# A residual loaded two tiles ahead, low-half products last in a chunk, and new figures in a build's own estimate

## The chip, the cores and the metric

The kernel runs on one core of one Trainium2 chip. Its time is the device time of one execution in microseconds (us), as the median of several runs. The profile is one further execution, recorded by the hardware profiler. TensorE (PE) does the matrix products, with its weight loads shown apart (PEld); VectorE (DVE), ScalarE (ACT) and GpSimd (POOL) do the elementwise work, and SyncE (SP) issues the transfers.

## The reference

Two blocks follow each other on 512 tokens of 2048 channels, all in float32. The first has a state-space branch, a differential attention and an attention to 256 memory tokens:

```python
h = rmsnorm(x, norm_pre); proj = h @ w_in            # 2048 -> 5120
y_s = gated(s5_scan(u_s, ...)); y_d = diff_attention(...) * silu(g_d)
y_x = memory_attention(q_x, mem_n, w_mem_kv) * silu(g_x)
mix = concatenate([y_s, y_d, y_x]) @ w_out
x = x + rmsnorm(mix, norm_post)
```

The last line is the residual that the change loads earlier. The second block has two layers over these 512 latent tokens and 256 context tokens; both streams use the same weights, and the attention of the latent tokens reads the keys of both:

```python
h = rmsnorm(x, g) * (1 + scale) + shift; hc = rmsnorm(xc, g) * (1 + scale_c) + shift_c
q, k, v, pool, fourier, gate = split(h @ w_in)       # q and k normalised and rotated
out = concatenate([attention, pool, fourier]) * silu(gate) @ w_out
x = x + gate_ada * out                               # and the context alike, in layer 0
return rmsnorm(x, final_norm_g)
```

## The kernel before, in words

Activations lie with channels on the partitions, as 16 tiles of 128 x 512 (or 128 x 256 for the context and the memory). A product in float32 is made of three products in a reduced format: each operand is split into a high half, which is a cast, and a low half, which is the rest (`hi`, `lo`). The three are hi x hi, hi x lo and lo x hi. In the profile `whi` and `wlo` are the halves of a weight chunk of 128 x 512, which serves four contraction tiles, and `hh` and `hl` are the halves of an activation tile. ScalarE casts `whi`, VectorE subtracts to get `wlo`; the chunk comes by DMA into `raw`. `gemm` (line 515) makes one output tile of 128 channels from two or four chunks, 12 matmuls each, into the PSUM tile `mm`. There are 912 chunks in a plan made at the start, and a chunk is split up to three chunks ahead of its use (`wsplit`, `wahead`).

All other work is written as generators, which run beside the products. Between matmuls `gemm` calls `tick`; `tick` advances each generator whose time has come on a clock of the build's own. This clock is not the chip's: `count` (line 286) adds to it an estimate for each instruction as it is recorded, from the table `COST` (line 217: a fixed part and a part per element for each engine) and a formula for matmuls. So the estimates set after how many products a step of other work stands in each engine's program. Each engine works its own program in that order; an instruction whose input is late holds up those behind it. Nothing of this clock is in the built program.

Steps that the text speaks of: `post` (line 1716) belongs to the second block. After the first block's output product it normalises the 16 output tiles, adds the residual (`xr`, loaded from `xT`), stores each tile (`x1d`) and scales it for layer 0. It runs beside the context products of layer 0. `attn_out` (line 846) transposes the softmax rows `P` into a PSUM tile `tp`, splits them into `pth` and `ptl`, and multiplies by the values into `pv`. `g_rope` (line 808) rotates queries and keys: four copies of 32 rows on ScalarE, then products on VectorE with the table `axial`. A read of one row in the profile always names line 210, where every operation is recorded; tiles tell the rows apart.

Of the kernel before, what the change touches and what calls it, by code (L numbers as in the profile page):

```python
# [22 lines left out]
N = 512  # L23
# [190 lines left out]

class Build:

    COST = {"vector": (0.08, 0.00106), "scalar": (0.09, 0.00084), "gpsimd": (0.15, 0.0021),
            "sync": (0.1, 0.00125), "tensor": (0.0, 0.0)}
    SLACK = 0.1
    CALM, LIMIT = 2.0, 3.6  # L220
# [5 lines left out]
    def __init__(self, tc, I, out):  # L226
        self.tc, self.I, self.out = tc, I, out
        self.nc = SimpleNamespace(**{e: Engine(self, e) for e in self.COST})
        self.free = dict.fromkeys(self.COST, 0.0)
        self.written, self.used, self.slot_free, self.rings = {}, {}, {}, {}  # L230
# [55 lines left out]
    def count(self, name, op, a, kw):  # L286

        aps = [x for x in (*a, *kw.values()) if hasattr(x, "tensor")]
        outs = [kw[k] for k in ("out", "accum_out") if kw.get(k) is not None] or [aps[0]]
        after = max([self.written.get(x.tensor.name, 0.0) for x in aps  # L290
                     if not any(x is o for o in outs)], default=0.0)
        after = max([after] + [self.slot_free.get(o.tensor.name, 0.0) for o in outs])
        size = max(math.prod(x.shape[1:]) for x in aps)
        fixed, per = self.COST[name]
        if name == "vector" and op == "tensor_scalar":
            per /= 2
        if name == "tensor":
            r = a[1].dtype == F32R
            cost = max(a[2].shape[-1], 256 if r else 128) / 2400.0 * (1 if r else 4) + 0.0027
            if op == "transpose":  # L300
                cost /= 2
            elif a[1].shape[-1] == 32:
                cost /= 4
            self.clock = end = max(self.clock, after) + cost
        else:
            f = kw.get("func")
            if f in (AF.Sin, AF.Tanh, AF.Exp) and (f == AF.Sin) != self.trig:
                self.trig = f == AF.Sin
                self.free[name] = max(self.free[name], self.clock) + 1.3
            if name == "scalar" and kw.get("accum_out") is not None:  # L310
                fixed += 0.09
            end = max(self.free[name], self.clock, after) + fixed + per * size
            self.free[name] = end
            end += 2.0 if name == "sync" else 0.2
        for o in outs:
            self.written[o.tensor.name] = end
        for x in aps:
            self.used[x.tensor.name] = max(self.used.get(x.tensor.name, 0.0), end)
        if not (name == "sync" and outs[0].space == DRAM):
            self.cur.ready = max(self.cur.ready, end)  # L320
# [194 lines left out]
    def gemm(self, name, mt, H, n, order, ahead=None):  # L515
        while len(self.live["mm"]) > 1 and (self.pmx is None or self.live["mx"]):
            self.tick(0.5)
        if len(self.live["mm"]) < 2:
            ps = self.t(self.pmm, "mm", [128, n], bufs=2)
            self.live["mm"].append(ps.tensor.name)  # L520
        else:
            ps = self.t(self.pmx, "mx", [128, n])
            self.live["mx"].append(ps.tensor.name)
        ks = lambda a: [order[a] * 4 + kk for kk in range(4)] if a < len(order) else []
        for a, ci in enumerate(order):
            if ahead is not None and a == 2:
                self.spawn(self.split_ahead(ahead))
            hi, lo = self.wget((name, mt, ci, n))
            while lo.tensor.name not in self.split_w:
                self.tick(0.3)  # L530
            while any(k not in H.ok for k in ks(a)):
                self.tick(0.3)
            H.need(ks(a) + (ks(a + 1) if self.wi > 1 else []))
            for kk in range(4):
                s = slice(kk * 128, kk * 128 + 128)
                self.mm3(ps, (hi[:, s], lo[:, s]), H[ci * 4 + kk],
                         a == 0 and kk == 0, a == len(order) - 1 and kk == 3)
                if kk < 3 or a < len(order) - 1:
                    self.tick()
        return ps  # L540

# [1138 lines left out]
    def block2(self):  # L1680
        nc, I = self.nc, self.I
# [5 lines left out]
        pp = self.pool("post1", es, bufs=1)  # L1687
# [28 lines left out]
        def post():  # L1716
            yield 12
            while self.alive([fc, *fs]):
                yield 0
            B0 = yield from self.g_bcast([acc, last[0]], N, D)  # L1720
            B = self.t(pp, "B", [128, N], bufs=2)
            yield
            nc.scalar.copy(B, B0)
            self.over(B0)
            yield
            xr = []
            for k in range(16):
                xr.append(self.t(pp, "xr", [128, N], bufs=2))
                self.load(xr[k], I["xT"][:, k])
                if k == 0:  # L1730
                    yield
                self.mul(X[k], X[k], B)
                self.add(X[k], X[k], xr[k])
                yield 3.0
                nc.sync.dma_start(out=self.x1d[k], in_=X[k])
                sq = acc if k == 0 else self.t(pp, "sq", [128, N], bufs=2)
                self.act(sq, X[k], AF.Square)
                yield 0.3
                if 0 < k < 15:
                    self.add(acc, acc, sq)  # L1740
            B0 = yield from self.g_bcast([acc, sq], N, D)
            B = self.t(pp, "B", [128, N], bufs=2)
            yield
            nc.scalar.copy(B, B0)
            self.over(B0)
            yield
            for k in list(range(8, 16)) + list(range(8)):
                self.stt(X[k], X[k], self.G0_0[:, k:k + 1], B, ALU.mult, ALU.mult)
                HX.ok.add(k)
                yield 2.2  # L1750
                if k >= 8:
                    HX.need([k])

        fp = self.spawn(post())


# [446 lines left out]
```

## Time and profile before

| | before |
|---|---|
| median of 3 runs | 2883.99 us (2881.13 to 2885.41) |
| the profiled execution | 2885.97 us |
| its span, first to last instruction | 2884.2 us |
| mean granted TensorE clock | 0.978 of full speed |
| TensorE busy | 2740.9 us, 95% |
| VectorE busy | 1664.8 us, 58% |
| ScalarE busy | 1213.8 us, 42% |
| DMA | 412.73 MB, mean 143 GB/s |

An engine's busy time is the union of its instructions; a matmul's end is modelled, so that matmuls overlap in the rows, and the spacing of their starts says how fast they follow each other. The granted clock is the share of 2.4 GHz that TensorE was given; it has two levels, 1.2 and 2.4 GHz, so a stretch at 0.91 spent 18% of its time at the lower one. A wait is the idle time of an engine in front of an instruction, put down to what came last.

### The profile page before, as it was taken

The numbers are of one execution on the slowest core, as the hardware profiler recorded it, in microseconds if no ns is written. First come the engines' busy times: TensorE is split into PE (matmuls) and PEld (weight loads), VectorE is DVE, ScalarE is ACT, GpSimd is POOL, SyncE is SP. The second block draws the span as 40 slices with busy tenths as digits, with TensorE's granted clock in tenths as the row PEclk, the third lists the DMA queues.
The fourth block names the chain that finished last, engine by engine and source line by source line (L and its number), as shares of the span: only waits on it lengthen the run. The fifth ranks groups of instructions, "written<-read, shape, count | busy, mean of one in ns | idle before, by whom it ended". The sixth has DMA issues, their size and how long they took to land.

```text
span 2884.2 us, 46821 instructions
## 1 busy us (share of the span) xinstructions
PE 2740.9 (95%) x17390; PEld 2279.8 (79%) x17390; DVE 1664.8 (58%) x3696; ACT 1213.8 (42%) x2339; POOL 168.3 (6%) x338
## 2 busy tenths in 40 slices
PE   6899999999999988899999999999999999999997
PEld 5677788778777787898987888878877778888785
DVE  8756557766643366775555455555466654555433
ACT  4544335643442344544443444444344444444322
POOL 0234334000000000000000000000000000000001
PEclk9999999999999998999999999999999999999998
DMA  5445566565576666667632222225433222222343
GB/s 173 136 155 158 178 204 208 183 223 182 185 236 210 210 220 199 193 205 222 206 101 59 63 70 81 74 73 172 143 125 108 64 65 66 76 82 74 113 119 111
DMA packets 241621, 412.73 MB, mean 143 GB/s; under 512 B 35952, under 2 KB 51312, under 8 KB 241392
## 3 DMA queue, kind: packets, MB, share of 16 engines
q1 hardware_dynamic: 241392, 409.73, 45.2%
q8 instruction: 137, 2.24, 0.3%
q14 instruction: 92, 0.75, 0.1%
HBM read 382.36 MB, written 25.17 MB: 141 GB/s over the span
## 4 chain that ended last, share of the span: by engine, by line
PE 77%; issue 8%; DVE 8%; DMA 4%; ACT 2%; SPq 1%; POOL 0%; DVEq 0%; POOLq 0%; ACTq 0%
PE mm L210 62%; PE tp L210 7%; PE pv L210 4%; PE S L210 3%; DVE wlo L210 2%; DMA raw<-w_in 2%; PE V L210 2%; DVE hl L210 1%; DMA xr<-xT 1%; DMA raw<-w_out 1%; DMA raw<-w_kv 1%; DVE mx L210 1%; ACT whi L210 1%; SPq L210 1%; DVE rs_a L210 0%
## 5 line engine op out<-in xcount | busy, mean ns | idle before, releaser
L210 PE MATMUL mm<-hh,whi 128*128 128x512 f32 (+1 forms) x3648 | 1364.6, 374 | 27.4 <-ACT hh L210 23.9
L210 PE MATMUL mm<-hh,wlo 128*128 128x512 f32 (+1 forms) x3648 | 1333.2, 365 | 55.3 <-DVE wlo L210 55.3
L210 PE MATMUL mm<-hl,whi 128*128 128x512 f32 (+1 forms) x3648 | 1331.6, 365 | 8.0 <-DVE hl L210 7.5
L210 ACT CAST whi<-raw 128x512 fp32r<-128x512 f32 x912 | 563.1, 620 | 903.6 <-PE mm L210 663.9
L210 DVE TENSOR_TENSOR wlo<-raw,whi 128x512 fp32r<-128x512 f32 x912 | 622.6, 694 | 373.7 <-ACT whi L210 369.7
L210 PEld LDWEIGHTS mm<-hh,wlo 128*128 128x128 f32 x3648 | 702.4, 193 | 169.6 <-DVE wlo L210 62.2
L210 PEld LDWEIGHTS mm<-hh,whi 128*128 128x128 f32 x3648 | 702.9, 193 | 155.0 <-ACT hh L210 26.9
L210 PEld LDWEIGHTS mm<-hl,whi 128*128 128x128 f32 x3648 | 703.9, 193 | 110.8 <-DVE hl L210 13.6
L210 DVE TENSOR_TENSOR ptl<-tp,pth 128x512 fp32r<-128x512 f32 (+3 forms) x128 | 80.7, 630 | 111.7 <-ACT pth L210 111.7
L210 ACT CAST pth<-tp 128x512 fp32r<-128x512 f32 (+3 forms) x128 | 69.2, 540 | 161.7 <-PE tp L210 148.8
L210 PE MATMUL tp<-adaw,adac 128*32 128x128 f32 x3072 | 107.6, 281 | 5.1 <-DMA adaw<-ada 5.0
L210 PEld LDWEIGHTS tp<-adaw,adac 128*32 128x32 f32 x3072 | 79.8, 111 | 34.9 <-issue 24.6
L210 POOL MEMSET s<- 128x8 f32 x24 | 1.7, 106 | 1646.2 <-DVE xk9l L210 1053.5
L210 ACT COPY s<-mm 32x512 f32<-32x512 f32 (+3 forms) x124 | 66.5, 537 | 63.2 <-PE mm L210 62.0
L210 ACT ACTIVATE s<-mm 128x512 f32<-128x512 f32 (+1 forms) x80 | 41.8, 523 | 115.4 <-PE mm L210 115.4
L210 DVE TENSOR_TENSOR acc<-acc,sq 128x512 f32<-128x512 f32 (+1 forms) x70 | 44.6, 636 | 48.6 <-ACT sq L210 45.6
L210 PE MATMUL tp<-ident,P 128*128 128x128 f32 x448 | 69.2, 274 | 0.0
L210 DVE SCALAR_TENSOR_TENSOR s<-mm,vec,axial 128x512 f32<-128x512 f32 x20 | 15.0, 752 | 92.7 <-ACT s L210 92.7
L210 PEld LDWEIGHTS tp<-ident,P 128*128 128x128 f32 x448 | 56.0, 141 | 13.5
L210 POOL TENSOR_TENSOR bb<-bb,cm 128x192 f32<-128x192 f32 (+1 forms) x96 | 57.0, 594 | 7.5
L210 DVE SCALAR_TENSOR_TENSOR mx<-mm,adav,xr 128x512 f32<-128x512 f32 x32 | 24.0, 750 | 51.4 <-PE mm L210 51.4
L210 DVE SCALAR_TENSOR_TENSOR s<-s,mm 128x512 f32<-128x512 f32 (+1 forms) x48 | 28.7, 597 | 41.5 <-ACT s L210 41.1
(938 smaller groups left out, 2487.7 us busy)
## 6 DMA issues: line engine op xcount, KB each, us to landing
raw<-w_in SPq DMA_DIRECT2D x608, 256.0 KB, 2.8
adaw<-ada SPq DMA_DIRECT2D x384, 256.0 KB, 4.0
raw<-w_out SPq DMA_DIRECT2D x256, 256.0 KB, 3.0
raw<-w_kv SPq DMA_DIRECT2D x32, 256.0 KB, 3.4
mx<-xT SPq DMA_DIRECT2D x16, 256.0 KB, 4.3
bbd<-bb SPq DMA_DIRECT2D x16, 256.0 KB, 5.1
ccd<-bb SPq DMA_DIRECT2D x16, 256.0 KB, 4.9
bb<-bbd SPq DMA_DIRECT2D x8, 512.0 KB, 5.0
```

What stands on the lines that cost most here:

```text
L210: fn(*a, **kw)
```

## The change

Three edits. The figures of the estimate are set anew: the fixed part of a VectorE instruction from 0.08 to 0.16 us, of a ScalarE instruction from 0.09 to 0.2, a matmul of 512 columns in the reduced format from 0.216 to 0.227 us. In `gemm` the low-half products of a chunk stand behind the 8 others, and `tick` is called after each pair of products, so six times in a chunk where it was four. In `post` the residual has three buffers where it had two, and is loaded two tiles ahead.

```diff
-    COST = {"vector": (0.08, 0.00106), "scalar": (0.09, 0.00084), "gpsimd": (0.15, 0.0021),
+    COST = {"vector": (0.16, 0.00103), "scalar": (0.2, 0.00084), "gpsimd": (0.15, 0.0023),
             "sync": (0.1, 0.00125), "tensor": (0.0, 0.0)}
...
-            cost = max(a[2].shape[-1], 256 if r else 128) / 2400.0 * (1 if r else 4) + 0.0027
+            cost = (max(a[2].shape[-1], 236) + 32) / 2400.0 if r else max(a[2].shape[-1], 128) / 600.0
             if op == "transpose":
                 cost /= 2
             elif a[1].shape[-1] == 32:
-                cost /= 4
+                cost *= 0.31
...
+            end = a == len(order) - 1
             for kk in range(4):
-                s = slice(kk * 128, kk * 128 + 128)
-                self.mm3(ps, (hi[:, s], lo[:, s]), H[ci * 4 + kk],
-                         a == 0 and kk == 0, a == len(order) - 1 and kk == 3)
-                if kk < 3 or a < len(order) - 1:
+                w = hi[:, kk * 128:kk * 128 + 128]
+                for half in range(2):
+                    self.mm(ps, w, H[ci * 4 + kk][half], a == kk == half == 0, False)
+                self.tick()
+            for kk in range(4):
+                self.mm(ps, lo[:, kk * 128:kk * 128 + 128], H[ci * 4 + kk][0], False, end and kk == 3)
+                if kk % 2 and not (end and kk == 3):
                     self.tick()
...
             xr = []
+
+            def fetch():
+                xr.append(self.t(pp, "xr", [128, N], bufs=3))
+                self.load(xr[-1], I["xT"][:, len(xr) - 1])
+
+            fetch()
+            fetch()
+            yield
             for k in range(16):
-                xr.append(self.t(pp, "xr", [128, N], bufs=2))
-                self.load(xr[k], I["xT"][:, k])
-                if k == 0:
-                    yield
+                if k < 14:
+                    fetch()
                 self.mul(X[k], X[k], B)
                 self.add(X[k], X[k], xr[k])
```

The rows below are of the built programs' order, not of a trace; they hold no time. On TensorE, in layer 0 of the second block on the latent tokens, the end of the fifth query projection (`mm_17947`) before; `mm_18079` is the next product:

```order
L210 MATMUL mm_17947<-hh_3731_17223,wlo_17949 128x512
L210 MATMUL mm_18079<-hh_3098_14098,whi_17986 128x512
L210 MATMUL mm_18079<-hl_3099_14099,whi_17986 128x512
L210 MATMUL mm_18079<-hh_3098_14098,wlo_17987 128x512
L210 MATMUL tp_18088<-ident_90,P_17869 128x128
L210 MATMUL tp_18088<-ident_90,P_17905 128x128
L210 MATMUL tp_18088<-ident_90,P_17945 128x128
L210 MATMUL tp_18088<-ident_90,P_18004 128x128
L210 MATMUL pv_18026<-pth_18059,cv10h_11880 128x512
L210 MATMUL pv_18026<-ptl_18060,cv10h_11880 128x512
L210 MATMUL pv_18026<-pth_18059,cv10l_11881 128x512
L210 MATMUL mm_18079<-hh_3107_14135,whi_17986 128x512
```

The same place after the change: between the projection's last product and these rows stand 4 transposes, 3 attention products and the first 4 products of the next tile (here `mm_18078`).

```order
L210 MATMUL mm_18078<-hh_3124_14233,whi_17986 128x512
L210 MATMUL mm_18078<-hl_3125_14234,whi_17986 128x512
L210 MATMUL mm_18078<-hh_3134_14271,whi_17986 128x512
L210 MATMUL mm_18078<-hl_3135_14272,whi_17986 128x512
L210 MATMUL mm_18078<-hh_3104_14140,wlo_17987 128x512
L210 MATMUL mm_18078<-hh_3116_14183,wlo_17987 128x512
L210 MATMUL tp_18098<-ident_90,P_17874 128x128
L210 MATMUL tp_18098<-ident_90,P_17915 128x128
L210 MATMUL tp_18098<-ident_90,P_17953 128x128
L210 MATMUL tp_18098<-ident_90,P_18007 128x128
L210 MATMUL pv_18029<-pth_18072,cv10h_11821 128x512
L210 MATMUL pv_18029<-ptl_18073,cv10h_11821 128x512
```

The low-half products (`wlo`) now follow the eight others of the chunk, and the product that reads `ptl` stands 10 chunk products behind the projection's end where it stood 3.

On VectorE at the same place, before; `s<-mm,vec,axial` is the rotary product that reads the projection:

```order
L210 TENSOR_TENSOR ptl_18033<-tp_18027,pth_18032 128x512
L210 TENSOR_TENSOR wlo_18039<-raw_17989,whi_18038 128x512
L210 SCALAR_TENSOR_TENSOR s_18072<-mm_17947,vec_88,axial_17271 128x512
L210 TENSOR_TENSOR ptl_18060<-tp_18054,pth_18059 128x512
L210 SCALAR_TENSOR_TENSOR s_18071<-s_18071,vec_88,axial_17271 128x512
L210 TENSOR_TENSOR wlo_18081<-raw_18012,whi_18080 128x512
L210 TENSOR_TENSOR ptl_18094<-tp_18088,pth_18093 128x512
```

And after:

```order
L210 TENSOR_TENSOR ptl_18036<-tp_18030,pth_18035 128x512
L210 TENSOR_TENSOR wlo_18039<-raw_17989,whi_18038 128x512
L210 SCALAR_TENSOR_TENSOR s_18061<-mm_17945,vec_88,axial_17268 128x512
L210 SCALAR_TENSOR_TENSOR s_18060<-s_18060,vec_88,axial_17268 128x512
L210 TENSOR_TENSOR ptl_18073<-tp_18067,pth_18072 128x512
L210 TENSOR_TENSOR s_18061<-s_18061,s_18060 128x512
L210 TENSOR_TENSOR wlo_18080<-raw_18012,whi_18079 128x512
```

Both rotary products now stand ahead of the next `ptl`. At the following place of this form, one head later, a `wlo` stands between them and the `ptl` as well.

On SP's queue, the second and third load of the residual before, each in the step that uses it (`x1d` is the store of a finished tile, `raw` a weight chunk):

```order
L210 DMA x1d_80<-mx_2099_9474 128x512
L210 DMA xr_12003<-xT 128x512
L210 DMA raw_12014<-w_in 128x512
L210 DMA raw_12032<-w_in 128x512
L210 DMA x1d_80<-mx_2120_9580 128x512
L210 DMA raw_12062<-w_in 128x512
L210 DMA xr_12095<-xT 128x512
```

After, the first three loads:

```order
L210 DMA xr_11829<-xT 128x512
L210 DMA xr_11831<-xT 128x512
L210 DMA raw_11841<-w_in 128x512
L210 DMA raw_11862<-w_in 128x512
L210 DMA raw_11880<-w_in 128x512
L210 DMA pw_11896<-pw 128x512
L210 DMA dftc_11898<-dft_c 128x256
L210 DMA fw_11900<-fw 128x512
L210 DMA dftn_2599_11902<-dft_n 128x256
L210 DMA raw_11911<-w_in 128x512
L210 DMA xr_11919<-xT 128x512
```

Three tiles are on their way before the first store of a finished tile, which stands further on.

## Rows read from the trace of the kernel before

**Rows 1.** The page's first part: busy us, share, instructions.

```profile
PE 2740.9 (95%) x17390; PEld 2279.8 (79%) x17390; DVE 1664.8 (58%) x3696; ACT 1213.8 (42%) x2339; POOL 168.3 (6%) x338
```

**Rows 2.** Waits of TensorE, whole span: us in total, times, longest.

```profile
PE mm L210 <- DVE wlo L210: 55.3, 31, 6.1
PE mm L210 <- ACT hh L210: 23.9, 10, 8.6
PE pv L210 <- DVE ptl L210: 12.4, 4, 3.1
...
PE V L210 <- ACT mx L210: 3.6, 2, 3.2
```

**Rows 3.** Stretches: length, busy us by engine, granted clock, DMA share, GB/s.

```profile
8.00:96.00 88.00, 62.79 (x421) 58.77 (x422) 75.38 (x262) 44.89 (x97) 0.00 (x0) 0.88 0.54 170
...
1020.00:1185.00 165.00, 137.76 (x1206) 129.99 (x1205) 107.43 (x281) 70.81 (x160) 0.42 (x6) 0.91 0.64 210
1185.00:1240.00 55.00, 47.29 (x460) 44.27 (x460) 44.36 (x121) 26.57 (x55) 0.00 (x0) 0.97 0.56 177
```

**Rows 4.** Waits from 1020 to 1185 us, VectorE's and TensorE's.

```profile
DVE mx L210 <- DMA xr<-xT: 47.4, 16, 5.5
...
PE mm L210 <- DVE wlo L210: 23.3, 11, 3.8
```

**Rows 5.** The residual additions: ns minimum/median/maximum, first and last start.

```profile
L210 DVE TENSOR_TENSOR mx<-mx,xr x16: 691/692/694, 1031.0 to 1178.2; 128x512 f32<-128x512 f32 x16
```

**Rows 6.** VectorE in order of time: start, length, operation, idle before.

```profile
1111.74 0.69 DVE L210 TENSOR_TENSOR mx<-mx,xr 128x512 f32<-128x512 f32 x1 [5.36 <-DMA xr<-xT]
```

**Rows 7.** TensorE, 256 columns, two products at the full and two at the lower clock.

```profile
1052.23 0.28 PE L210 MATMUL mm<-hh,whi 128*128 128x256 f32 x1
1052.35 0.28 PE L210 MATMUL mm<-hl,whi 128*128 128x256 f32 x1
...
1053.55 0.41 PE L210 MATMUL mm<-hh,whi 128*128 128x256 f32 x1
1053.76 0.41 PE L210 MATMUL mm<-hl,whi 128*128 128x256 f32 x1
```

**Rows 8.** Wait of TensorE from 1185 to 1240 us.

```profile
PE mm L210 <- DVE wlo L210: 7.7, 5, 3.6
```

**Rows 9.** Wait of TensorE from 8 to 96 us.

```profile
PE mm L210 <- DVE wlo L210: 20.4, 9, 6.1
```

**Rows 10.** ScalarE in the rotary step of layer 0, in order of time.

```profile
1520.46 0.60 ACT L210 ACTIVATE s<-mm 128x512 f32<-128x512 f32 x1 [0.81 <-PE mm L210]
1521.08 2.34 ACT L210 COPY s<-mm 32x512 f32<-32x512 f32 x4
```

**Rows 11.** VectorE in the same step.

```profile
1523.45 0.75 DVE L210 SCALAR_TENSOR_TENSOR s<-mm,vec,axial 128x512 f32<-128x512 f32 x1 [5.69 <-ACT s L210]
1524.12 0.68 DVE L210 TENSOR_TENSOR ptl<-tp,pth 128x512 fp32r<-128x512 f32 x1
```

**Rows 12.** TensorE in the same step.

```profile
1520.96 0.60 PE L210 MATMUL tp<-ident,P 128*128 128x128 f32 x4
1521.32 0.48 PE L210 MATMUL pv<-pth,cv10h 128*128 128x512 f32 x1
1524.85 0.79 PE L210 MATMUL pv<-ptl,cv10h 128*128 128x512 f32 x1 [3.05 <-DVE ptl L210]
```

**Rows 13.** TensorE, 512 columns: two products, the second the fourth behind the first.

```profile
1499.58 0.39 PE L210 MATMUL mm<-hl,whi 128*128 128x512 f32 x1
...
1500.49 0.39 PE L210 MATMUL mm<-hh,wlo 128*128 128x512 f32 x1
```

**Rows 14.** Stretches of 10 us around three `ptl` waits; columns as in rows 3.

```profile
1523.00:1533.00 10.00, 8.15 (x31) 6.11 (x32) 5.28 (x9) 3.35 (x6) 0.00 (x0) 0.66 0.17 52
1574.00:1584.00 10.00, 7.94 (x30) 5.96 (x31) 5.07 (x8) 3.54 (x7) 0.00 (x0) 0.66 0.15 48
2317.00:2327.00 10.00, 8.79 (x40) 6.71 (x41) 6.57 (x18) 2.73 (x5) 0.00 (x0) 0.83 0.18 52
```

## The prediction

> **What bounds the kernel now.** I read the page's busy shares first: TensorE is busy 95% of the span, VectorE 58%, ScalarE 42% [rows 1]. So the time is TensorE's, and a change that leaves its instructions as they are can only take away its waits and the stretches in which it runs at the lower clock. Then the table of waits, TensorE alone, says for what it waited: 55.3 us for `wlo`, the low half of a weight chunk, in 31 waits; 23.9 us for `hh`, the high half of an activation tile; 12.4 us in 4 equal waits for `ptl` in the attention [rows 2]. The reader is to see that the low weight half is the largest item, though VectorE, which makes it, is idle 42% of the time. So I asked for the stretches. From 1020 to 1185 us, where the context products of layer 0 run beside `post()`, TensorE waits 23.3 us for `wlo`, and in the same stretch VectorE stands 47.4 us in front of one addition, 16 times, each time until the residual tile `xr` has landed [rows 4]. The granted clock there is 0.91 [rows 3]. One case: the addition starts at 1111.74 after 5.36 us of standing [rows 6]; every split queued behind it is late by as much.
>
> **The change part by part.** No matmul, split or transfer is added or taken away; the engines' programs keep their counts. Three edits move them.
>
> *A, the residual.* Before, `post()` issues each load directly ahead of the multiplication and the addition that uses it, so all 16 additions pay the transfer. Now two loads go out first, and the load of tile k+2 stands in step k. The 16 additions of before start between 1031.0 and 1178.2 us [rows 5], a step being some 9 us, so two steps are some 18 us, and the longest of the 16 waits is 5.5 us [rows 4]: the wait goes whole, 47.4 us of VectorE. The third buffer means that a load waits only for the addition of step k-1. What it is worth is read from TensorE: its 23.3 us [rows 4], and the lower clock after them. In the 165 us at 0.91 the granted clock was at its lower level for 2 x 0.09 x 165 = 30 us [rows 3]. At 2.4 GHz the 256-column products start 0.12 us apart, at 1.2 GHz 0.21 us [rows 7], so 44% of those 30 us was lost: 13 us. Together 36 us, if all of it goes. What is late next is VectorE itself: its 107.4 us of work in 165 - 36 = 129 us make it 83% busy. The nearest row for such a load without `xr` is 1185 to 1240 us: VectorE 44.4 of 55 us, 81% [rows 3], and there TensorE waits 7.7 us in 5 waits for `wlo` [rows 8]. At that rate 129 us would hold 18 us of waits again; the second edit cuts that (below) to about 10. I take 36 - 10 = 26 us; bounds 13 (36 less 18 and a third of that in clock) and 36.
>
> *B, low-half products last.* A chunk's 12 products were hi, hi, lo four times, so `wlo` was due 2 products after `whi`. Now it is due after 8. TensorE so has 6 more products to do before it can wait: 6 x 0.12 = 0.7 us with 256 columns [rows 7]. Of the 5 waits in [rows 8] the longest is 3.6, the other four are some 1 us each; 0.7 us off each leaves 4.2 of 7.7 us: 3.5 gained. At the start of the kernel (8 to 96 us) there are 9 such waits of 20.4 us [rows 9]; 0.7 us off each would be 6, but VectorE is busy there for 75.4 of 88 us [rows 3], and a product that no longer waits meets the next late split. I take 3 (0 to 6). Outside these three stretches 55.3 - 23.3 - 7.7 - 20.4 = 3.9 us are left, mostly in few waits; I take 2. B: 8.5 us (4 to 12). It costs something where the activations are late: a product pair now wants the next `hh`, `hl` after 2 products and not 3, and the 4 low products are left for the end. Where the last tile of a chunk arrives late, up to 3 products more follow it: 0.7 us at 512 columns. There are some seven places where a stage begins so (10 waits for `hh`, [rows 2]); most wait for the first tile alone. I take 2 us lost (0 to 5).
>
> *C, the build's estimates.* These numbers decide when work beside the products is called, and so after how many products it stands in TensorE's queue. The `ptl` waits show what a wrong order costs. At 1520.46 ScalarE begins a copy and then four copies of 32 rows, 2.34 us [rows 10]; VectorE's rotary product waits for the last of these, and the split `ptl` stands behind it [rows 11]; TensorE has reached the product that reads `ptl` and waits 3.05 us [rows 12]. The old estimate gave the four copies 4 x (0.09 + 0.43) = 2.08 us, the new one 2.52; VectorE's 512 columns, 0.68 to 0.75 us [rows 11], were 0.62 and are 0.69. For a product the trace has 0.91 us for four, 0.227 us each [rows 13]; the old figure was 0.216, the new (512 + 32)/2400 = 0.227. So the clock by which work is called now runs with TensorE's, and the work is credited with what it takes.
>
> In the order of the changed program the first of the two places of layer 0 still has the split behind the rotary products, two of them now, but in front of the product that reads it stand 10 chunk products, two sets of 4 transposes and 4 attention products, where 3 products, one set and 1 were. By [rows 12, 13] that is 10 x 0.227 + 2 x 0.36 (a set of transposes starts at 1520.96, the next product at 1521.32) + 4 x 0.23 = 3.9 us after the projection's last product, against 1.3 before; the split ends 0.7 us later. The wait falls from 3.05 to about 3.05 - 2.6 + 0.7 = 1.2 us. The second place has a chunk split between and dozens of products ahead: its wait goes. Both layers alike: 2 x 1.9 + 2 x 3.1 = 10 us. In 10 us around three of the four waits the granted clock is 0.66, 0.66 and 0.83 [rows 14]: 6.8, 6.8 and 3.4 us at the lower level. At the 44% of above that loses 7.5 us, of which I take 6. C: 16 us (6 to 18).
>
> A rule of the Trainium skill speaks against the new product figure: its page "TensorE: Matmul & The Clock Gate", section "Back-to-back issue gap", gives 512/2.4 + 2.5 = 216 ns for isolated 512-column products, which is the old figure, and 131 ns for a sustained stream. By either, the new figure would run the build's clock ahead of TensorE, and work would be called too early. The trace does not agree: 0.227 us [rows 13].
>
> *D, what the new order may do elsewhere.* A whole program is re-timed, and what it meets by chance is not to be read from before. The waits of before that came from work called a little too early, other than `ptl` (such as 3.6 us of scores for ScalarE's `mx`, [rows 2]), bound it: nothing at one end, a second set like C's at the other, 4 x 3.1 + 8 = 20 us lost. I take 3, nearest to the 3.6.
>
> **The sum.** 26 + 8.5 - 2 + 16 - 3 = 45.5 us. The profiled execution took 2885.97 us around a span of 2884.2; less 45.5 it would be 2840. The median of the three runs lies 2 us below the profiled one, so 2838.
>
> **The rivals.**
> *VectorE is the limit of the context stage* (0.16). Its 83% come in bursts, and the wait for `xr` only hid a queue that is full anyway. For it: the 7.7 us at 81%, and the first 96 us, where it is busy 86% and TensorE waits a fifth of the time. Against it: the smaller bursts now fit into the 0.7 us. Then A is 13, B 4, C 12, less 5: 24 us, 2860.
> *The residual is still late* (0.03): its loads sit on SP's queue behind weight loads that wait for VectorE. Against it, in the order shown, the first two loads stand ahead of nine other transfers. Then A is nothing: 2884 - 20 = 2864.
> *Called into the rotary step* (0.04), the one that ends slower: the new figures let the attention's split fall behind the four copies of most heads, not of two in each layer. There are 20 rotary products with this form, each collision at its old distance costs 3.1 us and some 2 us of clock. From 6 collisions on it eats the other 30 us (26 + 8.5 - 5); with 16 the time is 2884 - 30 + 80 = 2934. Against it: the order of the changed program shows the close sequence once in a layer.
> *By the skill's gap of 216 ns* (under 0.01, the trace having 0.227): each call would come 0.13 us too early for a chunk of 12 products, and C's four waits would stay; 2838 + 16 = 2854.
>
> **How the numbers follow.** My forecast, some 45 us gained, has 0.76. The range is 2808 to 2868 for 8 in 10: 36 + 12 + 18 = 66 us at the best ends gives 2818, and 10 more is left for a program that is re-timed whole; at the other end 2868 takes in the first two rivals. About 0.2% (6 us) is what a measurement of this kernel can tell from none. Only the rotary case, or all low ends with D's 20 us, come near to no gain or a loss: faster 0.91, same 0.04, slower 0.05.
>
> **What would show it.** A: VectorE's wait for `xr` is gone from the table of waits, and the stretch between the first and last residual addition is 30 us shorter at a clock of 0.95 or more. B: TensorE's total for `wlo` falls from 55 to some 33 us, half of it in the first 96 us. C: of the four waits of 3 us for `ptl` two are left, near 1 us. D: no new line over 5 us in TensorE's waits. I am wrong if `wlo` still stands above 45 us, or if waits for `pth`, `ptl` or `P` grow.

## The result, and the profile after

| | before | after |
|---|---|---|
| median (lowest to highest), 4 runs each | 2883.45 us (2881.13 to 2885.41) | 2841.77 us (2839.74 to 2842.71) |
| ratio of times, 95% interval | | 0.9861 [0.9848, 0.9874] |
| span of the profiled execution | 2884.2 us | 2840.9 us |
| mean granted TensorE clock | 0.978 | 0.984 |

The kernel is some 42 us faster; 45.5 were forecast, and 2838 us for the median. The first part of the page after the change, against [rows 1]:

```profile
PE 2730.0 (96%) x17390; PEld 2263.8 (80%) x17390; DVE 1662.9 (59%) x3696; ACT 1201.0 (42%) x2339; POOL 163.5 (6%) x338
```

The same 17390 products are busy 10.9 us less, for which the higher clock is the likely cause, and the rest of the span's 43.3 us, 32.4, is TensorE's idle time that is gone. The waits of TensorE over the whole span, against [rows 2] (us in total, times, longest):

```profile
PE mm L210 <- ACT hh L210: 26.4, 12, 7.8
PE mm L210 <- DVE wlo L210: 23.0, 16, 5.5
...
PE tp L210 <- DMA adaw<-ada: 6.9, 4, 6.1
...
PE pv L210 <- DVE ptl L210: 3.6, 4, 1.4
```

The wait for `adaw` is not new; before the change it was:

```profile
PE tp L210 <- DMA adaw<-ada: 5.0, 1, 5.0
```

The `wlo` line fell from 55.3 to 23.0 us and the `ptl` line from 12.4 to 3.6. By totals alone all three edits seem to have done what was said of them. Where each gain fell is read from stretches. Four loads into tiles called `xr` mark the stages: of `xT` (the context products of layer 0 begin), of `ctxT` (the context's output, then layer 0 of the latent tokens), of `x1d` (layer 1) and of `x2d` (the end). Between the first loads of before (length, busy us by engine, clock, DMA share, GB/s):

```profile
0.00:1025.50 1025.50, 971.26 (x7434) 778.30 (x7435) 634.71 (x1494) 444.16 (x906) 159.40 (x310) 0.98 0.59 188
1025.50:1325.50 300.00, 261.71 (x2364) 249.07 (x2362) 206.71 (x534) 141.26 (x313) 0.42 (x6) 0.94 0.63 202
1325.50:1952.20 626.70, 617.01 (x3348) 519.60 (x3349) 340.29 (x695) 262.01 (x469) 0.56 (x8) 0.99 0.34 102
1952.20:2693.10 740.90, 720.92 (x3490) 592.96 (x3489) 409.91 (x857) 312.16 (x567) 0.56 (x8) 0.99 0.32 97
2693.10:2884.20 191.10, 170.01 (x761) 139.84 (x759) 73.17 (x121) 54.22 (x88) 7.39 (x6) 0.95 0.39 121
```

And of after:

```profile
0.00:1033.70 1033.70, 976.03 (x7380) 778.22 (x7381) 635.20 (x1492) 441.40 (x906) 154.54 (x310) 0.98 0.58 185
1033.70:1299.90 266.20, 248.20 (x2354) 236.50 (x2352) 206.08 (x533) 137.89 (x314) 0.41 (x6) 0.99 0.70 226
1299.90:1917.20 617.30, 613.13 (x3412) 517.22 (x3413) 339.74 (x696) 259.12 (x468) 0.56 (x8) 1.00 0.35 108
1917.20:2650.40 733.20, 722.68 (x3489) 592.09 (x3489) 408.88 (x857) 308.72 (x566) 0.55 (x8) 0.99 0.32 98
2650.40:2840.90 190.50, 169.96 (x761) 139.79 (x759) 73.04 (x121) 53.85 (x87) 7.40 (x6) 0.95 0.39 122
```

The number of products in a stage is not the same: 3348 and 3412 in the third. The program has 3072 small products of `adaw`, the weights of the second block's scale and shift, which are called beside everything else and slide between stages. The same stretches for the instructions of `adaw` alone, before (length, busy us of TensorE and of its weight loads, clock, DMA):

```profile
0.00:1025.50 1025.50, 85.76 (x2496) 63.40 (x2496) 0.98 0.59 188
1025.50:1325.50 300.00, 17.49 (x448) 13.17 (x448) 0.94 0.63 202
1325.50:1952.20 626.70, 4.33 (x128) 3.25 (x128) 0.99 0.34 102
```

And after:

```profile
0.00:1033.70 1033.70, 84.39 (x2432) 61.56 (x2432) 0.98 0.58 185
1033.70:1299.90 266.20, 15.13 (x448) 11.37 (x448) 0.99 0.70 226
1299.90:1917.20 617.30, 6.48 (x192) 4.87 (x192) 1.00 0.35 108
```

I take these off each stage, as if each cost the time that it is busy. So read, the start became 9.6 us longer (949.3 against 939.7), the context stage 31.4 shorter (251.1 against 282.5), the context's output and layer 0 11.6 shorter, layer 1 7.7 shorter, the end 0.6. Nearly three quarters of the gain is in the context stage, and something was lost at the start. Each stage length comes from one execution; in the third set of runs below the kernel before alone lies between 2876 and 2891 us, so a difference of a few us in one stage is a hint and no more. In the stretch of [rows 3], and in the first 200 us in two parts:

```profile
8.00:96.00 88.00, 63.49 (x428) 57.84 (x428) 74.90 (x250) 47.35 (x100) 0.00 (x0) 0.92 0.57 180
96.00:200.00 104.00, 93.83 (x501) 71.73 (x501) 67.30 (x154) 47.23 (x95) 40.04 (x69) 0.92 0.44 135
1020.00:1185.00 165.00, 152.20 (x1474) 143.90 (x1473) 130.13 (x359) 81.49 (x186) 0.56 (x8) 0.99 0.73 240
```

In the third row the clock is 0.99 where it was 0.91, and VectorE does 130 us of work in the time in which it did 107. Its waits for `xr` are no longer listed there. What waits now in 1020 to 1200 us, against [rows 4]:

```profile
ACT whi L210 <- DMA raw<-w_in: 52.2, 27, 5.1
...
PE mm L210 <- DVE wlo L210: 4.4, 5, 1.6
```

ScalarE stands before the weight chunks' arrival, with the DMA engines 73% busy from 1020 to 1185 us; in that stretch its wait is 44.7 us where it was 32.8. The stream of weights may be the next limit of this stage; no run here tests that. The residual additions, against [rows 5]:

```profile
L210 DVE TENSOR_TENSOR mx<-mx,xr x16: 691/692/695, 1040.2 to 1166.4; 128x512 f32<-128x512 f32 x16
```

They take 126 us from first to last, where they took 147. The rotary place of [rows 10 to 12] in layer 0, in order of time, ScalarE first, then VectorE, then TensorE:

```profile
1496.22 2.34 ACT L210 COPY s<-mm 32x512 f32<-32x512 f32 x4
...
1498.60 0.75 DVE L210 SCALAR_TENSOR_TENSOR s<-mm,vec,axial 128x512 f32<-128x512 f32 x1 [3.85 <-ACT s L210]
...
1499.27 0.74 DVE L210 SCALAR_TENSOR_TENSOR s<-s,vec,axial 128x512 f32<-128x512 f32 x1
...
1499.93 0.68 DVE L210 TENSOR_TENSOR ptl<-tp,pth 128x512 fp32r<-128x512 f32 x1
...
1500.67 0.51 PE L210 MATMUL pv<-ptl,cv10h 128*128 128x512 f32 x1 [0.94 <-DVE ptl L210]
```

The split still stands behind the rotary products, as the order said, and TensorE waits 0.94 us where 1.2 was worked out and 3.05 had been.

### The profile page after: what moved, and what is told of

Its sections match the earlier page's. It is cut to its first block, busy times and chain, and to the rows that moved or that the text cites. A ratio compares the mean times of both kernels' runs of the same rounds, so it can differ in the third digit from the quotient of the medians.

```text
span 2840.9 us, 46797 instructions
## 1 busy us (share of the span) xinstructions
PE 2730.0 (96%) x17390; PEld 2263.8 (80%) x17390; DVE 1662.9 (59%) x3696; ACT 1201.0 (42%) x2339; POOL 163.5 (6%) x338
## 4 chain that ended last, share of the span: by engine, by line
PE 80%; issue 8%; DVE 5%; DMA 4%; ACT 2%; POOL 0%; SPq 0%; POOLq 0%; ACTq 0%; DVEq 0%
PE mm L210 65%; PE tp L210 7%; PE pv L210 4%; DMA raw<-w_in 3%; PE S L210 2%; PE V L210 2%; DVE wlo L210 1%; ACT whi L210 1%; DMA adaw<-ada 1%; DVE hl L210 1%; DVE mx L210 1%; ACT hh L210 0%; DVE s L210 0%; DMA raw<-w_kv 0%; DVE e_p L210 0%
## 5 line engine op out<-in xcount | busy, mean ns | idle before, releaser
L210 PE MATMUL mm<-hh,whi 128*128 128x512 f32 (+1 forms) x3600 | 1309.2, 371 | 32.4 <-ACT hh L210 26.4
L210 PE MATMUL mm<-hl,whi 128*128 128x512 f32 (+1 forms) x3600 | 1289.2, 366 | 7.6 <-DVE hl L210 6.9
L210 PE MATMUL mm<-hh,wlo 128*128 128x512 f32 (+1 forms) x3600 | 897.9, 367 | 23.0 <-DVE wlo L210 23.0
L210 PEld LDWEIGHTS mm<-hh,whi 128*128 128x128 f32 x3600 | 688.8, 191 | 155.6 <-ACT hh L210 31.1
L210 PEld LDWEIGHTS mm<-hl,whi 128*128 128x128 f32 x3600 | 689.0, 191 | 119.3 <-DVE hl L210 19.0
L210 PEld LDWEIGHTS mm<-hh,wlo 128*128 128x128 f32 x3600 | 629.6, 191 | 134.1 <-DVE wlo L210 26.9
L210 PEld LDWEIGHTS tp<-ident,P 128*128 128x128 f32 x448 | 55.6, 140 | 13.7
L210 DVE TENSOR_TENSOR adaa<-adaa,tp 128x128 f32<-128x128 f32 x72 | 20.4, 284 | 47.2 <-PE tp L210 47.2
```

The lines of the kernel that those rows point to most:

```text
L210: fn(*a, **kw)
```

## The experiments

All times are medians, with lowest and highest in brackets; ratios are against the kernel before on the same chip. Three sets were run, with the kernel before at 2883.72, 2882.58 and 2881.05 us.

**The residual alone** (edit A: of the change's diff the part in `post`; four calls of other work in a chunk as before).

> The residual two tiles ahead alone, in the order and with the estimates of before. My theory (term A): the context stage loses its 23.3 us of waits for wlo behind xr and the clock they cost, less what VectorE's own bursts leave: 23 to 29 us gained, near 2857. Rival, VectorE is the limit there: 10 to 15 us, near 2871. Rival, the residual lands late all the same: VectorE's wait for xr stays above 30 us and the time is 2883.

Measured: 2858.61 us (2849.30 to 2868.62, 4 runs), ratio 0.9899 [0.9868, 0.993]. TensorE's wait for `wlo` between 1000 and 1300 us:

```profile
PE mm L210 <- DVE wlo L210: 13.7, 12, 3.2
```

Between 999 and 1319 us, the same stage, it was before:

```profile
PE mm L210 <- DVE wlo L210: 31.3, 17, 3.8
```

From 1020 to 1185 us it is 13.5 us (23.3 before, [rows 4]), and the clock there 0.94 (0.91 before). The context stage is 22.7 us shorter (259.8 us without `adaw`), layer 0 and the start stay within a microsecond. VectorE's wait for `xr` is 1.5 us, once. The edit's own cause is so confirmed, in its place and near the size expected. Its runs spread over 19 us, more than any other kernel's; layer 1 was 6.5 us longer in the profiled one, the slowest of the four, and why is open.

**Edit B as a whole: low-half products last, with six calls in a chunk** (of the change's diff the part in `gemm`).

> The low-half products last and the six ticks alone. My theory (term B less its cost): 4 to 9 us gained, near 2877, TensorE's wait for wlo between 40 and 48 us, VectorE's wait for xr still 47. Rival, the slack of six products alone takes most of the wlo waits: wlo below 30 us, time near 2862, and then A and B overlap. Rival, re-timing by the ticks decides: the ptl waits or the first 200 us change by more than 5 us.

Measured: 2870.28 us (2864.61 to 2873.34, 5 runs), ratio 0.9949 [0.9929, 0.9968]. By the ratio that is 9 to 20 us, more than the 4 to 9 expected, and the trace puts it elsewhere: `wlo` fell only from 55.3 to 43.9 us, while the waits for `ptl`, which this edit was not to touch, are as good as gone, as the last rival said:

```profile
PE mm L210 <- DVE wlo L210: 43.9, 23, 6.1
...
PE pv L210 <- DVE ptl L210: 2.8, 4, 0.7
```

**The estimates alone** (edit C: the lines of the change's diff with `COST` and `cost`; four calls and the products as before).

> The estimates alone. My theory (term C less D): the four ptl waits fall from 12.4 to below 5 us, 10 to 16 us gained, near 2870; wlo waits stay near 55 us. Rival, the new figures move work by chance: ptl gains are there but the first 740 us or the context stage lose as much, time within 6 us of 2883. Rival, the ptl waits went by the ticks and not by the figures: ptl stays at 12 us here.

Measured: 2874.91 us (2870.72 to 2878.99, 7 runs), ratio 0.9968 [0.9952, 0.9983]. The waits for `ptl` are not gone, and a new one of 6 us has come:

```profile
PE pv L210 <- DVE ptl L210: 9.5, 4, 3.1
...
PE tp L210 <- DVE ptl L210: 6.0, 1, 6.0
```

What is gained lies mostly elsewhere. The start, all instructions:

```profile
0.00:1012.10 1012.10, 965.43 (x7317) 774.30 (x7318) 632.63 (x1491) 443.19 (x907) 151.55 (x310) 0.98 0.58 187
```

The same stretch, `adaw` alone:

```profile
0.00:1012.10 1012.10, 81.73 (x2368) 60.03 (x2368) 0.98 0.58 187
```

Without `adaw` that is 930.4 us, 9.4 less than before; before 1010 us the wait for `hh` fell from 12.0 to 3.4 us. Layer 0 is 5.0 us shorter, layer 1 2.9, the context stage 3.6 longer.

**The residual and edit B together**, both as above.

> The residual ahead and the low-half products last, with the estimates of before. If A and B add up: 2884 - 26 - 6.5, near 2851, and the estimates are worth the 9 to 10 us that are left to the changed kernel's 2842. If they overlap (both take away the same wlo waits): no more than the better of the two alone. If the estimates are needed for both to pay: above 2860.

Measured: 2836.41 us (2835.34 to 2838.70, 4 runs), ratio 0.9834 [0.9813, 0.9854]. Without the estimates the time is no worse than that of the whole change, and by the runs' ranges some 5 us better; the two intervals just overlap. It is 15 us below the 2851 expected if A and B add up; that B alone had gained more than its forecast explains a part of it.

**Edit B taken apart: the order of the products alone.** The low halves stand last, and other work is called after every third product, four times in a chunk as before.

```diff
+            P = [(hi, kk, j) for kk in range(4) for j in range(2)] + [(lo, kk, 0) for kk in range(4)]
+            for n_, (w, kk, j) in enumerate(P):
+                self.mm(ps, w[...], H[ci * 4 + kk][j], ...)
+                if n_ % 3 == 2 and not (end and n_ == 11):
+                    self.tick()
```

> The low-half products last, but work beside the products is called after every third product, four times in a chunk as before; residual and estimates as before. Theory, the order is what shortened the latent layers in the run with both: the ptl waits stay below 4 us and the time is near the 2870 of that run. Rival, the finer calling is what did it: the ptl waits are back near 12 us, the layers back at 516 and 519 us, and the time is within 6 us of 2883. In both, wlo waits fall by some 5 us.

Measured: 2879.61 us (2874.64 to 2884.23, 10 runs), ratio 0.9995 [0.9982, 1.0007]: nothing that can be measured. Yet the waits for `wlo` fell by 12.8 us. The waits of TensorE over its whole span:

```profile
PE mm L210 <- DVE wlo L210: 42.5, 23, 6.1
PE mm L210 <- ACT hh L210: 22.5, 11, 8.6
PE pv L210 <- DVE ptl L210: 13.8, 6, 3.1
PE mm L210 <- DVE hl L210: 8.5, 14, 1.9
PE mm L210 <- DVE s L210: 7.4, 2, 4.2
```

A new line for `s` (7.4 us), and more for `ptl`, stand against them. In the context stage, where `wlo` fell from 31.3 to 24.6 us, the stage is no shorter (285.1 us without `adaw`, 282.5 before): the new line for `s`, 7.4 us, lies whole in it, and VectorE still stands 50.2 us for `xr` there. In this one execution, 6.9 us shorter than the profiled one of before, the start is 7.9 us shorter and layer 0 4.2, layer 1 3.2 longer.

**Edit B taken apart: six calls alone**, with the products in the order of before.

```diff
+            P = [(w, kk, j) for kk in range(4) for w, j in ((hi, 0), (hi, 1), (lo, 0))]
...
+                if n_ % 2 == 1 and not (end and n_ == 11):
+                    self.tick()
```

> The products in the order of before (hi, hi, lo), but work beside them is called after every second product, six times in a chunk. Theory, the finer calling shortened the latent layers: the ptl waits fall below 5 us, layers near 505 and 514 us, time near 2872. Rival, the order did it: ptl stays near 12 us and the time is within 6 us of 2883. The wlo waits stay near 55 us in both.

Measured: 2860.14 us (2859.03 to 2861.73, 4 runs), ratio 0.9933 [0.9918, 0.9948]. This is the whole of edit B's gain, and no smaller. Waits of TensorE:

```profile
PE mm L210 <- DVE wlo L210: 50.4, 26, 7.3
...
PE pv L210 <- DVE ptl L210: 2.8, 4, 0.7
```

And VectorE's wait for the residual, which stays, since edit A is not in:

```profile
DVE mx L210 <- DMA xr<-xT: 46.5, 14, 7.6
```

The stages from `ctxT` and from `x1d`:

```profile
1322.60:1931.20 608.60, 604.73 (x3224) 511.43 (x3224) 338.29 (x690) 262.45 (x469) 0.55 (x8) 1.00 0.34 100
1931.20:2666.30 735.10, 720.93 (x3486) 593.12 (x3485) 409.77 (x857) 311.97 (x566) 0.56 (x8) 0.99 0.32 97
```

There are no `adaw` products left in either. Against 622.4 and 740.9 us before, they are 13.8 and 5.8 us shorter, and the start 4.9: in edit B the latent layers' gain comes from the finer calling. The programs' orders say how. At the two rotary places of layer 0, between a projection's last product and the product that reads `ptl`, there stand 3 and 3 chunk products before, 3 and 3 with the new product order alone, 14 and 14 with six calls alone. With the estimates alone the first place has 3 as before, and only the second has more; a new wait for `ptl`, 1.71 us, stands at a third place there, at 1634.5 us.

**The estimates taken apart**, on top of the residual and edit B. First the matmul's figure alone (the lines with `cost` in the change's diff):

> Residual ahead, low halves last, and of the estimates only the matmul's (0.227 in place of 0.216 for 512 columns). The run with neither figure gave 2836, the changed kernel 2842. Theory: the longer matmul figure runs the build's clock ahead, so work is called after fewer products, and alone, without the larger figures for the other engines, it brings back waits: 2840 to 2850. Rival: it is the figure that the trace shows and costs nothing: 2833 to 2838.

Measured: 2847.07 us (2846.16 to 2848.64, 4 runs), ratio 0.9888 [0.9873, 0.9902].

Then the figures of VectorE, ScalarE and GpSimd alone (the line with `COST`):

> Residual ahead, low halves last, and of the estimates only those of VectorE, ScalarE and GpSimd. Theory: the larger fixed parts hold work back where VectorE is thought to be behind; the first 400 us end some 5 us later than with the old figures and the time is 2838 to 2846. Rival: they are what the trace shows and spare waits: below 2834.

Measured: 2853.95 us (2852.12 to 2856.03, 4 runs), ratio 0.9911 [0.9896, 0.9926]. Each half alone is slower than none (2836) and than both (2842; the first half's interval just touches that of both). The second lies above either forecast. The first loses 5.5 us in the start and 3.8 in layer 1, without `adaw` and against the kernel that has neither; the second 4.4 in the start, 9.6 in the context stage and 5.4 in layer 0. It is no sum of two effects, and no one place.

**The residual with the estimates**, four calls, products as before.

> Residual ahead and the new estimates, with the products and the four calls of before. If the two add up as they were alone (25 and 9 us): near 2849, and the latent layers stay near 516 and 520 us, since the finer calling is missing. Rival, the estimates are worth nothing once the residual is ahead: near 2858; or they cost, as they did on top of the other two edits: above 2862.

Measured: 2840.11 us (2835.30 to 2842.66, 4 runs), ratio 0.9855 [0.9828, 0.9882]. By the ratios the estimates are worth some 13 us on top of the residual with four calls (0.9855 against 0.9899, the intervals just overlap), and cost some 8 on top of residual and edit B (0.9861 against 0.9834). Its start is 8.7 us shorter than before, its context stage some 34 and layer 0 6.5, layer 1 is as long as before (740.3 us), and its waits for `ptl` are still 9.5 us. This kernel has nothing of edit B and is as fast as the changed one (0.9861 [0.9848, 0.9874]). Against its trace the changed kernel's latent layers are 12.1 us shorter and its start is 18.3 us longer (949.3 against 931.0).

**A better version: the residual and six calls**, products and estimates as before.

```diff
+                if n_ % 2 == 1 and not (end and n_ == 11):
+                    self.tick()
...
+                if k < 14:
+                    fetch()
```

> Residual ahead and work beside the products called after every second product, with the products in the order of before and the estimates of before. If the two effects add up (25 us and 22 us when each was alone): near 2836, no worse than the run with the low halves last as well, so that the reorder of the products is worth nothing. Rival, the low halves last cover VectorE's bursts once the residual is ahead: 2842 to 2850, with 10 us more of wlo waits in the context stage than the 5.7 us of that run.

Measured: 2830.74 us (2828.93 to 2832.69, 4 runs), ratio 0.982 [0.9798, 0.9842], below the whole interval of the changed kernel. Its first three stages:

```profile
0.00:1027.20 1027.20, 972.39 (x7578) 777.06 (x7582) 636.37 (x1500) 443.14 (x907) 155.58 (x310) 0.99 0.59 193
1027.20:1294.40 267.20, 250.62 (x2353) 238.15 (x2345) 208.26 (x532) 139.63 (x312) 0.42 (x6) 0.98 0.69 221
1294.40:1903.20 608.80, 604.83 (x3224) 511.45 (x3224) 338.72 (x690) 262.79 (x469) 0.56 (x8) 1.00 0.33 100
```

The context stage and the latent layers gain what the changed kernel gains, and the start does not lose. From 1000 to 1300 us `wlo` is 8.8 us in the old order of products, as the changed kernel's 8.9 in the new one.

**A call after every product**, twelve in a chunk, with the residual.

```diff
-                if n_ % 2 == 1 and not (end and n_ == 11):
+                if not (end and n_ == 11):
                     self.tick()
```

> As the run before it, but work beside the products is called after every product, twelve times in a chunk. If finer calling is what pays, a little more of it pays a little more: 2826 to 2836. Rival, after every second product it is fine enough, and the rest is how the order happens to fall: 2836 plus or minus 8.

Measured: 2839.86 us (2837.45 to 2841.75, 4 runs), ratio 0.9851 [0.9829, 0.9873]. The other stages stay within 2 us of the six calls' (without `adaw`), and the start is 5.2 us longer. Here finer is better only up to six calls; the runs' ranges lie apart, the intervals just overlap.

**Finer steps at the start**: the residual and six calls, with one more `yield` in the middle of three polynomial loops on VectorE.

```diff
+            if n == 3:
+                yield
```

> Residual ahead, six calls in a chunk, products in the order of before, and in the preparation of the state-space coefficients the bursts of 24 to 31 small VectorE operations are cut in two, so that weight splits pass between them. Theory, the start is limited by those bursts (waits of 4.7 and 5.5 us for wlo, and the clock behind them): the first 96 us lose 6 to 10 us and the kernel 5 to 10, near 2830. Rival, the start is limited by VectorE's sum of work: what is gained by 96 us is given back by 400 us, and the time is within 4 us of the run without the cut.

Measured: 2827.53 us (2826.26 to 2829.12, 4 runs), ratio 0.9809 [0.9787, 0.983]. It is the fastest of all, and clearly faster than the changed kernel; its 3 us over the version above are within what a measurement here can tell from none. The clock of its first 96 us rose from 0.90 to 0.94 against the version above, that of the next 104 us fell from 0.97 to 0.93, and the start is 1.6 us shorter: a gain of 5 to 10 us from finer steps is not borne out, as the rival said.

## Why the prediction was right, and where it was not

The time was right by 4 us, in part by luck: the residual's gain is shown, but the other terms were credited to the wrong parts of the change, and the terms do not add up as the sum took them.

| step | predicted, us gained | the edit alone, 95% interval |
|---|---|---|
| A, the residual | 26 (13 to 36) | 20 to 38 |
| B, low halves last | 8.5 less 2 | -2 to 5 |
| six calls in place of four, part of B's edit | not priced | 15 to 24 |
| C less D, the estimates | 16 less 3 | 5 to 14 |

**A held, and alone it was worth more than its working.** The wait for `xr` went. In the stretch from 1020 to 1185 us the clock rose from 0.91 to 0.94 alone and to 0.99 with the rest, and 13.5 us of `wlo` were left alone, 3.8 with the rest, where about 10 were reckoned. These 10 had been 18 before the help of edit B, so the same working gives A alone 18 us and not 26; it measured 20 to 38. The first rival, VectorE as the limit, had put A at 13 us; the ratio excludes that. The additions' stretch was to shrink by 30 us; it shrank by 21 in the changed kernel and by 44 with the edit alone (1031.6 to 1134.5 us). As their pace also hangs on when `post()` is called, this was a poor mark; the stage is the better one, 22.7 us shorter with the edit alone and 31.4 with the rest.

**B failed as a cause.** "0.7 us off each" wait counted what TensorE no longer waits for, and took each such microsecond as gained. The order alone took 12.8 us out of the line for `wlo`, and the time did not move; nor is there a gain from it on top of six calls (0.9949 against 0.9933) or of six calls and the residual (0.9834 against 0.982). The first 96 us were to give half of the fall; of 32.3 us the context stage gave 22.4 (31.3 to 8.9), of which A alone takes 17.6, and the whole start 8.7 (21.7 to 13.0). The line for `wlo` ended at 23 us, below the forecast 33, and this was no sign that B was right.

**C's sum was right, its owner was wrong.** The step read the new order word for word, 10 products where 3 were, and worked out 1.2 us for a wait that measured 0.94; two such waits are left in the layers, 0.9 us each, as forecast. Layers 0 and 1 gained 11.6 + 7.7 = 19.3 us where 16 were put. But the step gave the new distance to the estimates, because it compared the kernel before with all edits at once. With the estimates alone the first place still has 3 products and the waits keep 9.5 us, though the two layers became 7.9 us shorter (5.0 + 2.9); with six calls alone it has 14, the waits keep 2.8, and the layers are 19.6 us shorter. The sentence that failed is "So the clock by which work is called now runs with TensorE's, and the work is credited with what it takes": how often that clock is looked at mattered here. The text named the six calls in the description of the change and gave them no price.

On the rule weighed in the prediction: after the change nine products in a row start from 1496.55 to 1498.40 us, 0.23 us apart, so the new figure is nearer the truth here. By the Trainium skill, "TensorE: Matmul & The Clock Gate", "Back-to-back issue gap", the gap at 512 columns is 216 ns for an isolated product and 131 ns in a sustained stream; the trace agrees with neither, as before. Yet the truer figure alone made the kernel with A and B slower, 2847 against 2836 us.

**D was mis-sized.** It was put at 3 us; the start alone lost 9.6 us, where B's working had it gain 3. In its first 1010 us TensorE's wait for `hh`, first before and then after, rose while `wlo` fell:

```profile
PE mm L210 <- ACT hh L210: 12.0, 4, 8.6
PE mm L210 <- ACT hh L210: 18.2, 6, 7.8
```

The clock from 96 to 200 us is 0.92 where it was 0.97. The same estimates shortened the start by 9.4 us alone and by some 9 with the residual, both with four calls; on top of residual and edit B they make it 11.3 us longer (938.0 to 949.3). The bound of 20 us held.

**The sum took B and C as separate gains, and they are not.** By the ratios A, B and C alone gain 1.01, 0.51 and 0.32% of the time. A with B gains 1.66% and A with C 1.45%, in each case their sum within the intervals; all three gain 1.39% where the sum is 1.84%, 13 us more, which is just beyond what the intervals allow. On top of A and C, B is worth nothing that can be measured (0.9855 against 0.9861). That the sum of 45.5 us came within 4 us of the measured 41.7 is luck: the six calls had no price, A alone was worth more than its working, and the three together less than their parts. The residual and six calls gain 50 us (2881 to 2831), and what the changed kernel has beside them gives some 10 back. The rotary rival, slower than before, is excluded; so is that the residual stays late.

What stays open: why each half of the estimates costs more than both, why the estimates shorten the start with four calls and lengthen it with edit B, and where the order alone gives back what the line for `s` does not explain of its 12.8 us.

## What to carry to other kernels

Look for an engine with time to spare that stands at the head of its own queue for a transfer: here 47 us of VectorE's standing were worth some 25 us, and one more buffer with an earlier load was the cure. Where an edit does two things (here an order of products and the number of calls), price and run both apart, and run the edits in pairs too, since here the estimates and edit B each paid on top of the residual and together paid no more than one. Before a new order is credited to a cause, read the order with that cause alone. A fall in a line of waits is not a gain until the stage it stands in is shorter, and a stage is compared only after the work that slid in or out of it is taken off.

## What was not expected of the hardware

A wait's price is not its length. With six calls alone 9.6 of the 12.4 us of `ptl` waits went, and the two latent stages became 19.6 us shorter (13.8 + 5.8). Around three of them the clock had been at 0.66, 0.66 and 0.83 [rows 14]; the first of these stages ran at 0.99 before and at 1.00 after. How much of the rest is that and how much other waits is not separated.

VectorE's splits stood behind its additions while these waited 47.4 us for `xr` [rows 4], and came sooner once that wait was gone. The Trainium skill states the rule, in "PSUM — Partial Sum Buffer", "Engine vs sequencer instructions": the queues of ScalarE, VectorE and GpSimd are strict FIFO; for VectorE the trace agrees. What such a queue costs another engine when its head waits for a transfer is shown here: 17.6 us of TensorE's waits for `wlo` (31.3 to 13.7) and a stage 22.7 us shorter.
